# Gathering small products between longer dense runs, and a last output block scaled in three transfers

## The chip, the cores and the metric

The kernel runs on one core of one Trainium2 chip. The metric is the device time of one launch in microseconds. Before the change three runs took 757.4 to 757.57 us, with a median of 757.45.

Five engines work side by side, each through its own instructions in a fixed order: PE (TensorE, matrix products; PEld is its weight load), DVE (VectorE), ACT (ScalarE), POOL (GpSimd), and SP (SyncE), which issues nearly all transfers.

## The reference

One decoder layer over 512 tokens, with 16 meta tokens ahead of them (528 in all), a width of 1024, in float32. Attention with differential softmax (8 heads) and a chunked gated delta rule (8 heads) run side by side on the same normalised input:

```python
h = concatenate([meta, x])
hn = rms_norm(h, norm_w)
aq, ak, av, az, dq, dk, dv, dz, db, da, ga, gd = split(hn @ w_in)
# attention, two maps a head
p = softmax(causal(q k^T / 8));  o_a = (p[0] - lam * p[1]) @ v
y_a = (rms_norm(o_a) * c * silu(az)) @ w_branch_attn
# delta rule, chunks, each head
t_inv = inverse(unit lower triangle: m + eye)
u, w = t_inv @ (v * beta), t_inv @ (k * beta * exp(gc))
v_new = u_c - w_c @ state
o_c = qd_c @ state + a_c @ v_new
state = state * cd_c + kd_c^T @ v_new
y_d = (rms_norm(o_d) * silu(dz)) @ w_branch_delta
h = h + (sigmoid(ga) * y_a + sigmoid(gd) * y_d) @ w_out
out = rms_norm(h, final_norm_w)[meta tokens dropped]
```

## The kernel before

**Dense products.** The products with the big weights (`w_in`, the two branches, `w_out`) make most of PE's work. Operands are split into a high and a low part (`hnH`, `hnL`, `wh`, `wl`; for sums of blocks `sumH`, `sumL`), and each product is made as three passes, high x high, high x low, low x high (`PASSES`), with 256, 264 or 512 columns. The functions are `first_products`, `product`, `pair_of_blocks` and `pair_products`, called one after the other by the generator `dense`, and `rest_of_gates`.

**Small products.** Between dense passes stand fp32 products and transposes of 32 to 128 rows. They come from `attention` (its score products are dense passes; `combine` turns the softmax's two maps into one and multiplies by the values) and from `delta_pair`, which treats the heads of the delta rule in four pairs. Of a pair, `keys`, `values`, `products` and `queries` make operands; then the inverse of the unit triangles is solved on DVE for all diagonal blocks at once, in 62 dependent operations on `tmps` and `ts` (31 multiplications, 31 subtractions). What it reads comes through DRAM (`scrm`) into `room`; what it gives goes through `scrt` to `tds` and `tdms`. From `tdms` the meta tokens' block is transposed (`tdmt`), and PE multiplies `vrm` by it, which starts the state. `square` and others finish the inverse (`TM`, `MT`, the wide `TT`), and `steps` walks over the chunks: `kT` by the state `S`, on DVE `vin`, its product with `TT`, on ACT `u`, then `ktd` by `u` and on DVE the next `S`; `output` adds the queries' product and that of `u` with `AT`.

**What sets the order.** All order is made ahead of time by a planner (`Plan`). Each part of the work is a generator (a `Task`), which yields the engine it wants next, a slot of a buffer, or an event. `run` takes again and again the task that could begin first by the planner's own clock; of several, the one with the lower rank. Its clock adds up durations from `Engine.time`, latencies from one engine to another (`HOP`) and an estimate for transfers. The order in which tasks are taken is the order in which each engine executes. No engine steps past an instruction that waits: what stands behind it waits too. `delta_pair` runs at rank 0, ahead of the dense work in a tie.

**Buffers.** Six PSUM banks are shared by kinds (`pd` three, `pat` two, `pdl` two); other buffers have the counts in `SLOTS`.

**The end.** The last products are `project`, four blocks of 128 tokens by two halves of 512 columns. `finish` takes such a half from its bank: DVE adds the residual (into `xr`), ACT squares it and sums the squares, DVE weighs it by the final norm's weights (`weigh`, a task of its own of rank 2). When both halves of a block are there, POOL raises the mean square to -0.5, ACT scales the half o = 0 and DVE the half o = 1, and SP sends each out, 128x512 apiece. In the last block the second half is computed in two cuts of 256 columns.

All instructions that go through the helper `Engine` stand in the profile at its one line, L231, so groups and rows are told apart by their tiles.

Of the kernel before, what the change touches and what calls it, by code (L numbers as in the profile page):

```python
# [79 lines left out]
COLD = 10500  # L80


class Task:
    def __init__(self, gen, rank, time, src):
        self.gen, self.rank, self.time, self.src, self.want, self.slot = gen, rank, time, src, (), 0
        self.issued = None


class Plan:
# [9 lines left out]
    def __init__(self, slots, kinds, banks):  # L99
        self.free = dict.fromkeys((PE, DVE, ACT, POOL, SP), 0.0)  # L100
        self.slots = {k: [(0.0, SP, i) for i in range(n)] for k, n in slots.items()}
        self.slots["bank"] = [(0.0, SP, i) for i in range(banks)]
        self.kinds = dict(kinds)
        self.events, self.tasks = {}, []
        self.task, self.engine, self.end, self.arrival = None, None, 0.0, 0.0
        self.dma = self.hwdge = 0.0

    def here(self):

# [4 lines left out]
    def spawn(self, gen, rank=None):  # L114
        time, src = self.here() if self.task else (0.0, SP)
        self.tasks.append(Task(gen, self.task.rank if rank is None else rank, time, src))
# [21 lines left out]
    def transfer(self, nbytes):  # L138
# [2 lines left out]
        self.dma = max(self.dma, self.hwdge) + nbytes / 360 + 20  # L141
        self.arrival = self.dma + 900

    def resume(self, task, engine, begin):
        self.task, self.engine, self.end, self.arrival = task, engine, begin, 0.0
        task.want = next(task.gen, None)
        task.time, task.src = self.here()
        task.issued = self.end if self.arrival else None
        if engine:
            self.free[engine] = self.end  # L150
        if task.want is None:
            self.tasks.remove(task)
        self.task = self.engine = None
# [31 lines left out]
    def run(self):  # L185
        self.settle()
        while self.tasks:
            best = None
            for task in self.tasks:
                eng = task.want  # L190
                if isinstance(eng, tuple) or eng not in self.free:
                    continue
                t = task.time if task.issued is None or eng != SP else task.issued
                if task.src != eng:
                    t += self.HOP[task.src] + (80 if eng == PE else 0)
                elif eng in (DVE, ACT):
                    t += 130
                key = max(t, self.free[eng]), task.rank
                if best is None or key < best[0]:
                    best = key, task  # L200
            assert best, sorted({str(t.want) for t in self.tasks})
            self.resume(best[1], best[1].want, best[0][0])
            self.settle()


# [60 lines left out]
def hybrid_block(ctx: ExitStack, tc: tile.TileContext, x, meta, wblk, wbd, wout, pcol, prow, out):  # L266
# [45 lines left out]
    def tick(event, n):  # L312
        ticks[event] = ticks.get(event, 0) + 1
        if ticks[event] == n:
            done(event)
        return ticks[event] == n
# [670 lines left out]
    def delta_pair(gi):  # L987
# [258 lines left out]
        for o in range(4):  # L1246
# [2 lines left out]
            G.affine_select(out=part, in_=part, pattern=[[1, 32], [-3, 11]], base=-(o % 3),  # L1249
                            channel_multiplier=-1 if o == 3 else 0, compare_op=ALU.is_equal, fill=0.0)  # L1250
        yield name("scr")
        msub = room[1].rearrange("p a t -> p (a t)")[:, 0:D].rearrange("p (j i) -> p j i", i=32)
        for o in range(4):

# [258 lines left out]
    def attention(h):  # L1513
# [11 lines left out]
        def combine(i, st, es):  # L1525
            N = NM + P * (i + 1)
            yield DVE
            V.reciprocal(out=st[:, 5:6], in_=st[:, 4:5])
            yield DVE
            V.tensor_scalar(out=st[:, 6:7], in0=l0[:, i:i + 1], scalar1=st[:, 5:6], scalar2=nlam, op0=ALU.mult, op1=ALU.mult)  # L1530
            yield DVE
            V.scalar_tensor_tensor(out=es[0], in0=es[1], scalar=st[:, 6:7], in1=es[0], op0=ALU.mult, op1=ALU.add)
            give("e")

            yield ("pm",)
            which = plan.task.slot
            pm = late["pm"][which]
            yield ACT
            A.copy(out=pm[:, 0:2, 0:NM], in_=es[0][:, 0:NM].unsqueeze(1).broadcast_to([P, 2, NM]))
            yield DVE  # L1540
            V.tensor_tensor(out=pm[:, 2, 0:NM], in0=es[0][:, 0:NM], in1=pm[:, 0, 0:NM].bitcast(F32), op=ALU.subtract)
            yield ("pT",)
            pT, pmT = slot(ap, [P, NC, P], F32, "pT"), mk(ap, [96, P], F32R, "pmT", SLOTS["pT"])
            yield ("pat",)
            yield PE
            pt = bank("pat")
            for n in range(i + 1):
                T.transpose(pt[:, n * P:(n + 1) * P], es[0][:, chunk(n)], ident)
            give("e")
            w = (i + 1) * P  # L1550
            dst = pT[:, 0:i + 1, :].rearrange("p n q -> p (n q)")
            yield ACT
            A.copy(out=dst, in_=pt[:, :w])
            give("pat", pt)
            yield ("pat",)
            po = bank("pat")
            yield PE
            T.transpose(po[0:96, P:2 * P], pm.rearrange("p a t -> p (a t)").bitcast(F32), ident)
            plan.give("pm", which)
            yield ACT  # L1560
            A.copy(out=pmT, in_=po[0:96, P:2 * P])
            yield PE
            T.matmul(po[:, 0:P], pmT, late["vm"], start=True, stop=False)
            for n in range(i + 1):
                T.matmul(po[:, 0:P], pT[:, n, :], vs[:, n, :], start=False, stop=n == i)
            give("pT")
            yield ACT
            A.copy(out=o[:, i, :], in_=po[:, 0:P])
            A.activation(out=po[:, P:2 * P], in_=po[:, 0:P], func=AF.Square, accum_out=ss[:, i:i + 1])
            give("pat", po)  # L1570
            tick(f"ao{h}", NC)
# [52 lines left out]
        for c in range(NC):  # L1624
            yield ACT
            A.activation(out=o[:, c, :], in_=o[:, c, :], func=AF.Copy, scale=ss[:, c:c + 1])
        yield f"az{h}"
        yield ("pat",)
        yield PE
        pt = bank("pat")  # L1630
# [377 lines left out]
    def finish(hf, tb, c0, c1, pd, tag, ssq, fnw, xr):  # L2008
# [13 lines left out]
        def weigh():  # L2022
            yield DVE
            V.tensor_tensor(out=t, in0=t, in1=fnw[hf][:, c0:c1], op=ALU.mult)
            tick(f"fw{tb}", 3 if tb == NC - 1 else 2)

        spawn(weigh(), 2)

        if col == 0:
            yield DVE  # L2030
# [1 line left out]
        elif c1 == 512:  # L2032
# [4 lines left out]
            G.tensor_tensor(out=ssq[:, 4:5], in0=ssq[:, 4:5], in1=mhalf[:, 0:1], op=ALU.pow)  # L2037
            yield f"fw{tb}"

            def scale(o):  # L2040
                t = xr[o, tb]
                if o == 0:
                    yield ACT
                    A.activation(out=t, in_=t, func=AF.Copy, scale=ssq[:, 4:5])
                else:
                    yield DVE
                    V.tensor_scalar_mul(out=t, in0=t, scalar1=ssq[:, 4:5])
                yield SP
                S.dma_start(out=out[tb * P:(tb + 1) * P, 512 * o:512 * o + 512], in_=t)

            for o in range(2):
                spawn(scale(o))
        else:
            yield DVE
            V.scalar_tensor_tensor(out=ssq[:, 3:4], in0=ssq[:, col:col + 1], scalar=1.0 / D, in1=ssq[:, 3:4],
# [144 lines left out]
```

## Time and profile before

| | |
|---|---|
| median of 3 runs | 757.45 us |
| the profiled execution's own time | 757.24 us |
| span of its trace | 755.5 us |
| PE busy | 735.5 us, 97% of the span, 5311 instructions |
| PEld busy | 668.6 us, 88% |
| DVE busy | 626.2 us, 83% |
| ACT busy | 498.6 us, 66% |
| POOL busy | 74.7 us, 10% |
| granted clock of TensorE, mean | 0.997 of full |

The profile is of one execution; its time is 0.21 us below the median, and 1.74 us of it lie outside the span. A row of the trace has the start in us, the duration (of one instruction, or from the first's start to the last's end where several are drawn together as xN), the engine, the operation, what it writes and reads, and in brackets how long the engine stood still just ahead of it and for whom. In the view of stretches each row has the stretch, its length, then pairs of busy time and instructions for PE, PEld, DVE, ACT and POOL, then the granted clock, the share of the DMA engines and GB/s.

PE's matmuls are pipelined: the record of a pass lasts longer than the time from its start to that of the next one. That time from start to start is called a turn here: 0.12 us for a pass of 256 or 264 columns.

### The profile page before, as it was taken

Reading aid. Unit: us, or ns where it says so; the run is one execution under the profiler, and the core shown is the slowest. Engines: PE = TensorE matmul, PEld = TensorE weight load, DVE = VectorE, ACT = ScalarE, POOL = GpSimd, SP = SyncE. Lnnn points to the kernel's source line nnn. Section 1 sums busy time; section 2 is a strip of 40 time slices with the busy share of each in tenths; the row PEclk is TensorE's granted clock in tenths of the full one; section 3 lists DMA queues with packets and bytes.
Section 4 is the critical chain, followed back from the end, with each engine's and each line's share of the span. In section 5 each row is a group of like instructions: output and inputs, shape, how many; then the busy total and the mean of one; then the engine's idle time right before and its main releaser. Section 6 shows DMA issues by size and latency. Waiting matters only on the chain.

```text
span 755.5 us, 14370 instructions
## 1 busy us (share of the span) xinstructions
PE 735.5 (97%) x5311; PEld 668.6 (88%) x5311; DVE 626.2 (83%) x1431; ACT 498.6 (66%) x1322; POOL 74.7 (10%) x86
## 2 busy tenths in 40 slices
PE   5999999999999999999999999999999999999996
PEld 5998888899899899989989989988988998899875
DVE  6999999998889789879989888997479869797453
ACT  6369565879965678976767797767675445545132
POOL 3205000202000301100030210010000000000001
PEclk9999999999999999999999999999999999999998
DMA  8141321225314112521331152152141443132602
GB/s 306 57 133 33 114 80 64 64 71 158 97 42 140 34 53 85 169 78 52 110 79 59 36 180 85 56 202 65 49 147 57 141 130 121 56 118 90 239 4 109
DMA packets 45431, 74.88 MB, mean 99 GB/s; under 512 B 20728, under 2 KB 25636, under 8 KB 45360
## 3 DMA queue, kind: packets, MB, share of 16 engines
q1 hardware_dynamic: 45360, 73.95, 30.8%
q8 instruction: 42, 0.69, 0.4%
q14 instruction: 29, 0.24, 0.1%
HBM read 67.58 MB, written 6.36 MB: 98 GB/s over the span
## 4 chain that ended last, share of the span: by engine, by line
PE 83%; ACT 8%; DVE 4%; issue 2%; DMA 1%; POOL 0%; SPq 0%; POOLq 0%; ACTq 0%
PE bank L231 80%; PE psc L231 3%; ACT wh L231 2%; DVE wl L231 1%; ACT TM L231 1%; ACT ak L231 1%; DMA xt<-in_x_dram 1%; ACT vr L231 0%; DMA raw<-in_wblk_dram 0%; ACT bank L231 0%; ACT MT L231 0%; ACT e L231 0%; ACT aq L231 0%; ACT sqk L231 0%; DVE hnL L231 0%
## 5 line engine op out<-in xcount | busy, mean ns | idle before, releaser
L231 PE MATMUL bank<-hnH,wh 128*128 128x512 f32 (+4 forms) x664 | 233.4, 355 | 0.7 <-ACT hnH L231 0.7
L231 PE MATMUL bank<-hnH,wl 128*128 128x512 f32 (+4 forms) x664 | 221.6, 337 | 0.0
L231 PE MATMUL bank<-hnL,wh 128*128 128x512 f32 (+4 forms) x664 | 221.5, 337 | 0.0
L231 DVE TENSOR_TENSOR wl<-raw,wh 128x1024 fp32r<-128x1024 f32 (+1 forms) x120 | 134.9, 1126 | 24.6 <-ACT wh L231 24.1
L231 ACT CAST wh<-raw 128x1024 fp32r<-128x1024 f32 (+1 forms) x120 | 116.3, 971 | 43.4 <-PE bank L231 36.0
L231 PEld LDWEIGHTS bank<-hnH,wl 128*128 128x128 f32 x664 | 124.1, 188 | 13.9
L231 PEld LDWEIGHTS bank<-hnH,wh 128*128 128x128 f32 x664 | 124.5, 189 | 13.4 <-ACT hnH L231 0.9
L231 PEld LDWEIGHTS bank<-hnL,wh 128*128 128x128 f32 x664 | 124.4, 189 | 10.0
L231 PE MATMUL bank<-sumH,wh 128*128 128x264 f32 x224 | 68.5, 306 | 0.0
L231 PE MATMUL bank<-sumH,wl 128*128 128x264 f32 x224 | 63.6, 284 | 0.0
L231 PE MATMUL bank<-sumL,wh 128*128 128x264 f32 x224 | 63.5, 284 | 0.0
L231 DVE SCALAR_TENSOR_TENSOR y<-xp,pc,y 128x528 f32<-128x528 f32 (+1 forms) x72 | 54.0, 753 | 1.1 <-ACT y L231 1.0
L231 ACT ACTIVATE e<-psc,ast 128x144 f32<-128x144 f32 (+3 forms) x64 | 34.7, 543 | 21.5 <-DVE ast L231 18.3
L231 PEld LDWEIGHTS bank<-sumH,wh 128*128 128x128 f32 x224 | 42.3, 189 | 1.1 <-issue 0.6
L231 PEld LDWEIGHTS bank<-sumL,wh 128*128 128x128 f32 x224 | 42.4, 189 | 0.0
L231 PEld LDWEIGHTS bank<-sumH,wl 128*128 128x128 f32 x224 | 42.1, 188 | 0.0
L231 PE MATMUL bank<-btH,wh 128*128 128x256 f32 x128 | 36.1, 282 | 0.5 <-ACT sn L231 0.5
L231 PE MATMUL bank<-btH,wl 128*128 128x256 f32 x128 | 35.8, 280 | 0.0
L231 PE MATMUL bank<-btL,wh 128*128 128x256 f32 x128 | 35.8, 280 | 0.0
L231 ACT CAST wh<-st 128x1024 fp32r<-128x1024 f32 x22 | 23.1, 1048 | 13.0 <-PE bank L231 12.8
L231 PE MATMUL psc<-ak,aq 128*128 128x264 f32 (+3 forms) x160 | 29.7, 305 | 0.8 <-DVE aq L231 0.4
L231 DVE TENSOR_TENSOR wl<-st,wh 128x1024 fp32r<-128x1024 f32 x22 | 26.8, 1218 | 3.4 <-ACT wh L231 1.9
(373 smaller groups left out, 1699.5 us busy)
## 6 DMA issues: line engine op xcount, KB each, us to landing
raw<-in_wblk_dram SPq DMA_DIRECT2D x96, 512.0 KB, 3.5
raw<-in_wout_dram SPq DMA_DIRECT2D x8, 512.0 KB, 5.1
xt<-in_x_dram SPq DMA_DIRECT2D x4, 512.0 KB, 4.8
TM<-gcd SPq DMA_DIRECT2D x8, 256.0 KB, 5.2
xr<-in_x_dram SPq DMA_DIRECT2D x8, 256.0 KB, 6.3
out_dram<-xr SPq DMA_DIRECT2D x8, 256.0 KB, 2.5
room<-scrm SPq DMA_DIRECT2D x12, 128.0 KB, 3.3
oad<-room SPq DMA_DIRECT2D x6, 256.0 KB
```

The costliest lines, as they stand in the source:

```text
L231: return real(*args, **kw)
```

## The change

1. **The planner** (`Task`, `Plan`) learns which tasks are dense: those of the generators `dense`, `rest_of_gates` and `attention`, the last one only up to its closing transposes. When PE goes from small to dense work, 85 ns are added in the planner's clock (`SWITCH`). While a dense run lasts and another dense task is ready, a small product is not begun before the run has lasted 500 ns (rank 0) or 900 ns (`RUNS`). While small products run, a dense task is put 80 ns back in the comparison (`STAY`).
2. **`combine`**: of the sum over the values and the meta tokens' values, the meta tokens' product (`vm`, `pmT`) is made last; it was first.
3. **`delta_pair`**: the planner gets one more event to wait for, `t3`, before the fetch into `room`: a sum over token blocks, which lay in the same buffer, has then been split into its high and low part.
4. **`finish`**: the last 256 columns of the last block are no longer weighed by a task of their own; DVE weighs and scales them in one operation. The last block goes out in three transfers in place of two: the second half's first 256 columns, the first half, the last 256 columns.

The instructions of PE are the same in number and shape. POOL's and SP's are too, but for the one transfer more; DVE's end changes as under 4.

```diff
+DENSE = ("dense", "rest_of_gates", "attention")
+SWITCH, RUNS, STAY = 85, (500, 900), 80
 class Task:
+        self.other = False
 class Plan:
+        self.run_kind, self.run_since = False, 0.0
+    def dense(self, task):
+        return task.gen.__name__ in DENSE and not task.other
     def resume(self, task, engine, begin):
+        if engine == PE and self.dense(task) != self.run_kind:
+            self.run_kind, self.run_since = not self.run_kind, begin
+            begin += SWITCH * self.run_kind
     def run(self):
+            steady = self.run_kind and any(
+                t.want == PE and self.dense(t) and t.time + (t.src != PE) * (self.HOP[t.src] + 80) <= self.free[PE]
+                for t in self.tasks)
...
-                key = max(t, self.free[eng]), task.rank
+                if eng == PE and steady and not self.dense(task):
+                    t = max(t, self.run_since + RUNS[task.rank > 0])
+                begin = max(t, self.free[eng])
+                key = begin + STAY * (eng == PE and not self.run_kind and self.dense(task)), task.rank
                 if best is None or key < best[0]:
-                    best = key, task
+                    best = key, task, begin
-            self.resume(best[1], best[1].want, best[0][0])
+            self.resume(best[1], best[1].want, best[2])
...
         yield name("scr")
+        yield "t3"
         msub = room[1].rearrange("p a t -> p (a t)")[:, 0:D].rearrange("p (j i) -> p j i", i=32)
...
             yield PE
-            T.matmul(po[:, 0:P], pmT, late["vm"], start=True, stop=False)
             for n in range(i + 1):
-                T.matmul(po[:, 0:P], pT[:, n, :], vs[:, n, :], start=False, stop=n == i)
+                T.matmul(po[:, 0:P], pT[:, n, :], vs[:, n, :], start=n == 0, stop=False)
+            T.matmul(po[:, 0:P], pmT, late["vm"], start=False, stop=True)
...
         yield f"az{h}"
+        plan.task.other = True
...
-            tick(f"fw{tb}", 3 if tb == NC - 1 else 2)
-        spawn(weigh(), 2)
+            tick(f"fw{tb}", 2)
+        last = tb == NC - 1 and hf == 1 and c1 == 512
+        if not last:
+            spawn(weigh(), 2)
...
-            def scale(o):
-                t = xr[o, tb]
+            def scale(o, a, b):
+                t = xr[o, tb][:, a:b]
                 if o == 0:
                     yield ACT
                     A.activation(out=t, in_=t, func=AF.Copy, scale=ssq[:, 4:5])
+                elif last and a:
+                    yield DVE
+                    V.scalar_tensor_tensor(out=t, in0=t, scalar=ssq[:, 4:5], in1=fnw[o][:, a:b], op0=ALU.mult, op1=ALU.mult)
                 else:
                     yield DVE
                     V.tensor_scalar_mul(out=t, in0=t, scalar1=ssq[:, 4:5])
                 yield SP
-                S.dma_start(out=out[tb * P:(tb + 1) * P, 512 * o:512 * o + 512], in_=t)
+                S.dma_start(out=out[tb * P:(tb + 1) * P, 512 * o + a:512 * o + b], in_=t)
-            for o in range(2):
-                spawn(scale(o))
+            for o, a, b in ((1, 0, 256), (0, 0, 512), (1, 256, 512)) if last else ((0, 0, 512), (1, 0, 512)):
+                spawn(scale(o, a, b))
```

**The order at the steps over the chunks.** PE's order of before, in the first pair of heads (`u,AT` the output's second product, `S,kT` the next chunk's first, of the two heads in turn; `sumH`, `sumL` dense passes; the helper's line is L231 before and L252 now):

```order
L231 MATMUL bank_1_78<-u_1997,AT_1057 128x128
L231 MATMUL bank_2_79<-sumH_35_134,wh_23_120 128x264
L231 MATMUL bank_2_79<-sumL_39_138,wh_23_120 128x264
L231 MATMUL bank_2_79<-sumH_35_134,wl_24_121 128x264
L231 MATMUL bank_5_82<-S_2011,kT_549 128x128
```

Behind these rows stand once more the same three dense passes, and then the second head's `S,kT`. The same place in the changed kernel, with other dense passes beside it:

```order
L252 MATMUL bank_4_81<-u_1942,AT_1035 128x128
L252 MATMUL bank_2_79<-hnH,wh_19_116 128x264
L252 MATMUL bank_2_79<-hnL,wh_19_116 128x264
L252 MATMUL bank_2_79<-hnH,wl_20_117 128x264
L252 MATMUL bank_2_79<-hnH,wh_19_116 128x264
L252 MATMUL bank_2_79<-hnL,wh_19_116 128x264
L252 MATMUL bank_2_79<-hnH,wl_20_117 128x264
L252 MATMUL bank_5_82<-S_1961,kT_552 128x128
L252 MATMUL bank_6_83<-S_1964,kT_609 128x128
```

Six dense passes now stand in one run, and the two heads' small products together behind them. Over the whole order the runs of small products fall from 209 to 186, those of dense passes under 500 ns by the planner's clock from 37 to 4, and changes between products on a part and on the whole of PE's array from 92 to 90.

**The order at the solve's end.** In the first pair of heads, PE's product of `vrm` with the transposed `tdmt`, before:

```order
L231 MATMUL bank_5_82<-sumH_34_133,wl_20_117 128x264
L231 MATMUL bank_3_80<-vrm_673,tdmt_1612 32x128
L231 MATMUL bank_5_82<-sumH_34_133,wh_19_116 128x264
L231 MATMUL bank_5_82<-sumL_38_137,wh_19_116 128x264
L231 MATMUL bank_5_82<-sumH_34_133,wl_20_117 128x264
```

and now:

```order
L252 MATMUL bank_2_79<-hnH,wl_24_121 128x264
L252 MATMUL bank_4_81<-vrm_655,tdmt_1567 32x128
L252 MATMUL bank_6_83<-TM_662,MT_897 32x32 x4
L252 MATMUL bank_6_83<-TM_662,MT_962 32x32 x4
L252 MATMUL bank_6_83<-TM_662,MT_897 32x32 x4
L252 MATMUL bank_6_83<-TM_662,MT_962 32x32 x4
L252 MATMUL bank_5_82<-um_1669,ktm_654 128x128
```

The product was row 622 of PE's order and is row 589; small products of the same pair (`TM,MT` of `square`, `um,ktm` of the state) follow it at once, where dense passes did.

**The order in `combine`.** In one block of an attention head PE's order was, between two groups of dense passes:

```order
L231 MATMUL bank_3_80<-sumH_34_133,wh_23_120 128x264
L231 MATMUL bank_3_80<-sumL_38_137,wh_23_120 128x264
L231 MATMUL bank_3_80<-sumH_34_133,wl_24_121 128x264
L231 MATMUL bank_2_79<-vm_653,pmT_2898 128x128
L231 MATMUL bank_2_79<-vs_2623,pT_2897 128x128
```

and is now:

```order
L252 MATMUL bank_3_80<-sumH_36_135,wh_19_116 128x264
L252 MATMUL bank_3_80<-sumL_40_139,wh_19_116 128x264
L252 MATMUL bank_3_80<-sumH_36_135,wl_20_117 128x264
L252 MATMUL bank_6_83<-vs_2619,pT_2953 128x128
L252 MATMUL bank_6_83<-vm_635,pmT_2954 128x128
```

The product that needs ACT's copy `pmT` has changed places with that of the values, which needs the earlier copy `pT`.

## The prediction

> **What bounds the kernel now.** I read the page first: busy time, then the chain that ended last.
>
> ```profile
> span 755.5 us, 14370 instructions
> ...
> PE 735.5 (97%) x5311; PEld 668.6 (88%) x5311; DVE 626.2 (83%) x1431; ACT 498.6 (66%) x1322; POOL 74.7 (10%) x86
> ...
> PE 83%; ACT 8%; DVE 4%; issue 2%; DMA 1%; POOL 0%; SPq 0%; POOLq 0%; ACTq 0%
> ```
>
> PE is busy for 97% of the span and makes 83% of the chain. The change adds and removes no product: only time in which PE stands still can be won or lost. The table of stretches says where it stands still (time and instructions by engine; the first pair is PE).
>
> ```profile
> 30.00:530.00 500.00, 495.36 (x3816) 454.48 (x3817) 445.62 (x1105) 375.90 (x1086) 56.62 (x56) 1.00 0.29 89
> 530.00:748.90 218.90, 218.44 (x1350) 193.84 (x1349) 156.15 (x272) 106.90 (x206) 5.78 (x6) 1.00 0.32 105
> 748.90:755.50 6.60, 0.27 (x3) 0.07 (x1) 1.41 (x4) 1.23 (x3) 0.66 (x1) 0.70 0.31 117
> ```
>
> From 530 to 748.9 PE leaves 0.46 us, and the order of its work there is unchanged. Behind 748.9 lie 6.6 us of tail. From 30 to 530, where small products stand between dense ones, it leaves 4.64 us. The view of PE's waits in that stretch has eleven rows (what waited, for what, us, times, longest), 4.2 us in sum; these are the first, two that matter below, and the last:
>
> ```profile
> PE bank L231 <- DVE qT L231: 1.0, 2, 0.7
> ...
> PE bank L231 <- DVE tdmt L231: 0.4, 1, 0.4
> PE bank L231 <- DVE vin L231: 0.4, 1, 0.4
> ...
> PE bank L231 <- ACT cn L231: 0.2, 1, 0.2
> ```
>
> These understate it, since a matmul's record lasts longer than its turn. At the worst `vin`:
>
> ```profile
> 167.72 0.40 PE L231 MATMUL bank<-vin,TM 128*128 128x128 f32 x2
> 168.51 0.49 PE L231 MATMUL bank<-vin,TM 128*128 128x128 f32 x2 [0.39 <-DVE vin L231]
> ```
>
> A two-pass product takes 2 x 0.11 = 0.22 us of turn (pace below), the step is 0.79: 0.57 lost where the row says 0.39. With 0.18 more for each of the 13 named waits the pool is about 4.2 + 2.3 = 6.5 us.
>
> **The change part by part.** The sum is made against the profiled execution's own 757.24 us, 0.21 below the median 757.45.
>
> *Switches.* The planner now charges 85 ns whenever PE goes from small to dense products. Eight transposes between dense passes (start, length):
>
> ```profile
> 49.46 0.28 PE L231 MATMUL bank<-hnH,wl 128*128 128x256 f32 x1
> 49.58 1.04 PE L231 MATMUL bank<-ident,kT 128*128 128x128 f32 x8
> 50.37 0.36 PE L231 MATMUL bank<-hnH,wh 128*128 128x256 f32 x1
> 50.57 0.28 PE L231 MATMUL bank<-hnL,wh 128*128 128x256 f32 x1
> 50.69 0.28 PE L231 MATMUL bank<-hnH,wl 128*128 128x256 f32 x1
> ```
>
> The first dense record behind them is 0.08 longer (0.36 against 0.28), which looks like a price. By starts it is none: from 49.46 to 50.57 are 1.11 us, and one dense turn, eight of 0.11 and one dense make 0.12 + 0.88 + 0.12 = 1.12. [...] Only a product on a part of the array pays:
>
> ```profile
> 149.99 0.68 PE L231 MATMUL bank<-TM 64*64 64x64 f32 x8
> 150.59 0.39 PE L231 MATMUL bank<-hnH,wh 128*128 128x264 f32 x1
> 150.82 0.28 PE L231 MATMUL bank<-hnL,wh 128*128 128x264 f32 x1
> ```
>
> Eight records spread over 0.68 - 0.22 = 0.46 us are 0.06 each; 8 x 0.06 + 0.12 = 0.60, and 0.83 pass: 0.23. In the order, runs of small products fall from 209 to 186, but changes between a part and the whole of the array only from 92 to 90. So: 23 x 0 + 2 x 0.12 = **-0.2**, from 0 to 23 x 0.085 = -2.0.
>
> *Gathering.* At the steps over the chunks PE has six dense passes and then both heads' products, where it had three dense passes between the two (rows of PE's order, above). That lengthens some covers and shortens others. I add the paces along the order between a product and the one that needs its result. For `vin` the smallest cover rises from 0.44 to 0.89 us, but the median falls from 1.46 to 1.17; from `vin` to `u,ktd` the median goes from 1.17 to 1.25. Links with less cover than the shortest time that this kind of link took in the trace: 38 before, 32 now. I take **-1.0**, from -4 (over half of the pool) to +1.5 (the `vin` links late by 0.05 each).
>
> *Meta tokens' product behind.* It waited for ACT's copy `pmT`, here 131.12 - 130.82 - 0.12 = 0.18:
>
> ```profile
> 130.82 0.28 PE L231 MATMUL bank<-hnH,wl 128*128 128x264 f32 x1
> 131.12 0.33 PE L231 MATMUL bank<-vm,pmT 96*128 96x128 f32 x1
> ```
>
> Now `vs,pT`, which has its operands earlier, stands ahead with 0.22 a block. By such steps three or four of 32 blocks waited: **-0.4**, from 0 to -0.7.
>
> *The solve.* Each pair of heads solves its triangle on DVE: 62 dependent operations between DMAs, ended by a transpose for which PE's product `vrm,tdmt` waits; behind that, in order, all of PE's work. The first four rows are the DVE chains (own busy time last), the others the stretches on PE from the last `kT` product to `vrm,tdmt`:
>
> ```profile
> 89.33:128.40 39.07, 13.78 (x62) 1.00 0.25 82
> 212.58:255.20 42.62, 13.64 (x62) 1.00 0.21 69
> 345.53:384.90 39.37, 13.77 (x62) 1.00 0.23 75
> 472.91:506.70 33.79, 13.93 (x62) 1.00 0.37 127
> ...
> 72.29:136.68 64.39, 62.58 (x406) 55.97 (x404) 60.64 (x153) 40.23 (x99) 5.86 (x6) 1.00 0.30 86
> 198.33:263.56 65.23, 65.19 (x442) 59.72 (x441) 57.51 (x156) 44.18 (x120) 6.74 (x9) 1.00 0.24 67
> 331.96:392.46 60.50, 60.50 (x413) 55.32 (x411) 56.45 (x156) 39.44 (x114) 6.28 (x7) 1.00 0.29 82
> 458.81:514.40 55.59, 55.59 (x374) 50.57 (x372) 51.27 (x143) 36.35 (x100) 2.15 (x3) 1.00 0.35 109
> ```
>
> Before, other DVE rows inside the chains last 30.9, 36.8, 31.6 and 23.1 us by their own durations; in the new order 29.3, 29.3, 32.8 and 33.3. The chains took 0.87 of own plus others (154.9 of 177.5), so they change by -1.4, -6.5, +1.0 and +8.8. PE's work by paces on the same stretches was 61.0, 64.7, 59.9 and 55.3 and is now 59.8, 56.4, 57.5 and 59.6: -1.3, -8.3, -2.4, +4.3. Chain minus cover: -0.1, +1.8, +3.4, +4.5. There was next to no reserve except in pair 3:
>
> ```profile
> 513.34 0.19 DVE L231 STREAM_TRANSPOSE tdmt<-tdm 32x32 f32<-32x32 f32 x1
> ...
> 514.39 0.40 PE L231 MATMUL bank<-vrm,tdmt 32*32 32x128 f32 x2
> ```
>
> 514.39 - 513.53 = 0.86 of reserve there; pair 0 waited (the `tdmt` row above). So PE is late by up to 1.8 + 3.4 + 3.7 = 8.9 us, and at best wins back 0.8, which pairs 0 and 1 wait now. In pair 0 that product stands 33 rows earlier in PE's order, and where a dense pass followed it, now the 32x32 products follow at once: a little more of PE's work hangs on the transpose. Other DVE work that falls into gaps of the chain costs nothing (in pair 3 DVE stood idle for 55.59 - 51.27 = 4.3), so I take under a third of the upper end: **+2.5**, from -0.8 to +8.9.
>
> *Tail.*
>
> ```profile
> 750.35 0.42 DVE L231 TENSOR_TENSOR xr<-xr,fnw 128x256 f32<-128x256 f32 x1
> 750.51 0.66 POOL L231 TENSOR_TENSOR ssq<-ssq,mhalf 128x1 f32<-128x1 f32 x1 [4.20 <-DVE ssq L231]
> 751.21 0.72 ACT L231 ACTIVATE xr<-xr,ssq 128x512 f32<-128x512 f32 x1 [0.97 <-POOL ssq L231]
> 751.21 0.49 DVE L231 TENSOR_SCALAR xr<-xr,ssq 128x512 f32<-128x512 f32 x1 [0.44 <-POOL ssq L231]
> 751.72 0.81 SPq L231 DMA_DIRECT2D out_dram<-xr  x2
> ```
>
> The weighing that goes (0.42) ended at 750.77, beside POOL's power (to 751.17): nothing. DVE then has a half scaling, between 0.16 and 0.49, say 0.33, and 0.42: ready at 751.54 and 751.96, ACT's at 751.93. SP issues in 0.81 / 2 = 0.40 each: 751.57, 751.97, 752.37. The last issue is 0.25 later than now and carries half the bytes: **0**, from -0.4 to +0.4. The wait on `t3` is for a sum on DVE that was long done when the fetch went out: 0; uncovered it would delay that fetch, and with it the chain of a pair, by one sum, about the 1.1 us of this row:
>
> ```profile
> L231 DVE TENSOR_TENSOR wl<-raw,wh 128x1024 fp32r<-128x1024 f32 (+1 forms) x120 | 134.9, 1126 | 24.6 <-ACT wh L231 24.1
> ```
>
> Sum: -0.2 - 1.0 - 0.4 + 2.5 + 0 = +0.9: 758.1 us; against the median 757.45 + 0.9 = 758.3.
>
> **Rivals.**
>
> *Covered (faster).* The longer runs take most of the short waits, and DVE's fillings fall into gaps: -0.2 - 4.0 - 0.6 + 0.5 = -4.3: 753.1. For it: 38 falls to 32, the smallest `vin` cover doubles. Against it: the median of `vin` falls.
>
> *The solve late (slower).* PE's cover for the transpose is short by two thirds of the upper end, +6, less 1 of short waits: 762.4. It decides from 1 us a pair. For it: no reserve in pairs 0 to 2, and the 85 ns are charged 76 times on these four stretches (6.5 us) though full-array rows show no such price. Against it: before, the planner hit this product to within 0.9 us in all pairs.
>
> *It does not gather.* 209 to 186 runs is little, and the waits stay as they are: 757.2.
>
> **How the numbers follow.** Forecast 0.42, covered 0.27, late 0.21, no gathering 0.10. What measurement of this kernel tells from no change is about 0.2%, 1.5 us. The forecast's own spread (-2.5 to +4) puts 0.05 faster, 0.20 same and 0.17 slower; covered 0.26 faster, 0.01 same; late all slower; no gathering 0.01 faster, 0.09 same. Faster 0.32, same 0.30, slower 0.38. The range 752.8 to 763.5 leaves out the outer part of both rivals.
>
> **What would show it.** PE idle from 30 to 530 against 4.64 us; the rows of waits for `tdmt` (right: 2 to 4 us over the four pairs; under 1 us and the solve step is wrong); waits for `vin` and `u`, smaller in number; `pmT` gone; dense turns still 0.12 across a switch; the last issue near 752.4 less the shift of the span. Wrong altogether if another engine holds PE: a new long wait for `wl`, `xp` or `vT`.

## The result, and the profile after

The changed kernel takes 770.83 us (median of 4 runs, 767.92 to 771.0); the kernel before took 757.42 beside it. The ratio is 1.0168 (95% interval 1.0144 to 1.0192): 13 us slower. The profiled execution took 770.9, in a span of 769.2. The page of after, the same three parts as before the change (busy time, chain):

```profile
span 769.2 us, 14348 instructions
...
PE 742.8 (97%) x5311; PEld 671.4 (87%) x5311; DVE 625.7 (81%) x1431; ACT 498.1 (65%) x1322; POOL 75.0 (10%) x86
...
PE 58%; DVE 23%; ACT 10%; issue 4%; DMA 2%; POOL 1%; SPq 1%; DVEq 0%; POOLq 0%; ACTq 0%
```

PE has the same work and is "busy" 7.3 us longer; its share of the chain falls from 83% to 58%, and DVE's rises from 4% to 23%. The view of stretches, cut at the same places of the program as before (500, 218.9 and 6.6 us then):

```profile
30.00:543.60 513.60, 503.44 (x3839) 458.96 (x3838) 445.53 (x1109) 376.58 (x1096) 57.06 (x56) 0.99 0.29 86
543.60:762.60 219.00, 218.54 (x1331) 193.21 (x1331) 155.95 (x268) 105.87 (x198) 5.75 (x6) 1.00 0.32 106
762.60:769.20 6.60, 0.35 (x4) 0.15 (x2) 1.33 (x4) 1.23 (x3) 0.55 (x1) 0.83 0.26 94
```

All of the loss lies in the first one: 13.6 us. PE's idle time there is 513.60 - 503.44 = 10.16, against 4.64: 5.5 more. The other 8.1 are in PE's "busy" time. PE's waits in that stretch, the five longest of twelve rows, which make 9.8 us in sum (what waited, for what, us, times, longest):

```profile
PE bank L252 <- DVE tdmt L252: 3.6, 3, 1.5
PE bank L252 <- DVE vT L252: 1.1, 3, 0.5
PE bank L252 <- DVE xp L252: 1.1, 2, 0.9
PE bank L252 <- ACT ao L252: 0.9, 2, 0.5
PE psc L252 <- ACT e L252: 0.8, 3, 0.3
```

About half of those 8.1 shows in the column of the granted clock (third from the end) in fine stretches behind the solve of the first pair of heads:

```profile
132.00:134.00 2.00, 1.18 (x10) 0.76 (x8) 2.00 (x4) 2.00 (x9) 0.00 (x0) 1.00 0.00 0
134.00:136.00 2.00, 1.60 (x36) 1.37 (x35) 1.92 (x6) 1.94 (x6) 0.00 (x0) 0.86 0.68 178
136.00:138.00 2.00, 2.00 (x8) 1.77 (x9) 1.67 (x3) 1.89 (x6) 0.00 (x0) 0.50 0.24 92
...
144.00:146.00 2.00, 2.00 (x12) 2.00 (x12) 0.86 (x3) 0.85 (x3) 0.00 (x0) 0.58 0.18 70
146.00:148.00 2.00, 2.00 (x25) 1.77 (x24) 0.50 (x2) 1.63 (x2) 0.00 (x0) 1.00 0.00 0
```

For 10.2 us (135.44 to 145.68) TensorE ran at half its clock, which never happened in the profile of before between 30 us and its last products. What stands just ahead of it on PE (start, length):

```profile
132.53 0.28 PE L252 MATMUL bank<-hnH,wl 128*128 128x264 f32 x1
133.64 0.40 PE L252 MATMUL bank<-vrm,tdmt 32*32 32x128 f32 x2 [0.82 <-DVE tdmt L252]
133.98 1.09 PE L252 MATMUL bank<-TM,MT 32*32 32x32 f32 x32
135.01 0.48 PE L252 MATMUL bank<-um,ktm 32*128 32x128 f32 x2
135.88 0.79 PE L252 MATMUL bank<-um,ktm 32*128 32x128 f32 x2 [0.40 <-DVE um L252]
136.60 0.59 PE L252 MATMUL bank<-hnH,wh 128*128 128x264 f32 x1
```

From 132.65 to 136.60 PE has nothing but products on 32 of the array's 128 rows, with two stalls between. They are the gathered products of the solve's hand-over; in the order of before dense passes stood between them. The three runs that took 770.76 or more had a mean clock of 0.992, the one that took 767.92 had 0.997. So there are two losses to tell apart: waits, and the clock.

### The profile page after: what moved, and what is told of

It is laid out like the page before. It is cut to its first block, busy times and chain, and to the rows that moved or that the text cites. A ratio compares the mean times of both kernels' runs of the same rounds, so it can differ in the third digit from the quotient of the medians.

```text
span 769.2 us, 14348 instructions
## 1 busy us (share of the span) xinstructions
PE 742.8 (97%) x5311; PEld 671.4 (87%) x5311; DVE 625.7 (81%) x1431; ACT 498.1 (65%) x1322; POOL 75.0 (10%) x86
## 4 chain that ended last, share of the span: by engine, by line
PE 58%; DVE 23%; ACT 10%; issue 4%; DMA 2%; POOL 1%; SPq 1%; DVEq 0%; POOLq 0%; ACTq 0%
PE bank L252 56%; DVE wl L252 6%; PE psc L252 3%; DVE y L252 2%; ACT wh L252 2%; DVE ts L252 2%; DVE tmps L252 2%; DVE ast L252 2%; ACT TM L252 1%; DVE raw L252 1%; ACT e L252 1%; DVE ak L252 1%; DMA xt<-in_x_dram 1%; DVE qT L252 1%; DVE vT L252 1%
## 5 line engine op out<-in xcount | busy, mean ns | idle before, releaser
L252 PE MATMUL bank<-hnH,wh 128*128 128x512 f32 (+4 forms) x664 | 233.2, 354 | 3.0 <-DVE vT L252 1.1
L252 PE MATMUL bank<-hnH,wl 128*128 128x512 f32 (+4 forms) x664 | 222.1, 338 | 0.0
L252 PE MATMUL bank<-hnL,wh 128*128 128x512 f32 (+4 forms) x664 | 222.0, 338 | 0.0
L252 ACT CAST wh<-raw 128x1024 fp32r<-128x1024 f32 (+1 forms) x120 | 116.2, 971 | 45.8 <-PE bank L252 42.9
L252 DVE TENSOR_TENSOR wl<-raw,wh 128x1024 fp32r<-128x1024 f32 (+1 forms) x120 | 134.2, 1120 | 11.5 <-ACT wh L252 10.8
L252 PEld LDWEIGHTS bank<-hnH,wh 128*128 128x128 f32 x664 | 125.0, 190 | 17.0 <-DVE vT L252 2.2
L252 PEld LDWEIGHTS bank<-hnH,wl 128*128 128x128 f32 x664 | 124.7, 189 | 13.9
L252 PEld LDWEIGHTS bank<-hnL,wh 128*128 128x128 f32 x664 | 125.0, 190 | 9.5
L252 PE MATMUL bank<-sumH,wh 128*128 128x264 f32 x224 | 68.1, 304 | 0.1
L252 PE MATMUL bank<-sumL,wh 128*128 128x264 f32 x224 | 64.5, 288 | 0.0
L252 PE MATMUL bank<-sumH,wl 128*128 128x264 f32 x224 | 64.4, 287 | 0.0
L252 DVE SCALAR_TENSOR_TENSOR y<-xp,pc,y 128x528 f32<-128x528 f32 (+1 forms) x72 | 54.8, 762 | 0.5 <-ACT y L252 0.5
L252 ACT ACTIVATE e<-psc,ast 128x144 f32<-128x144 f32 (+3 forms) x64 | 34.5, 542 | 20.7 <-DVE ast L252 13.9
L252 PEld LDWEIGHTS bank<-sumH,wh 128*128 128x128 f32 x224 | 43.2, 193 | 0.5 <-ACT vT L252 0.3
L252 PEld LDWEIGHTS bank<-sumL,wh 128*128 128x128 f32 x224 | 43.3, 193 | 0.0
L252 PEld LDWEIGHTS bank<-sumH,wl 128*128 128x128 f32 x224 | 43.0, 192 | 0.0
L252 PE MATMUL bank<-btH,wh 128*128 128x256 f32 x128 | 36.3, 284 | 0.5 <-ACT sn L252 0.5
L252 PE MATMUL bank<-btH,wl 128*128 128x256 f32 x128 | 36.0, 281 | 0.0
L252 PE MATMUL bank<-btL,wh 128*128 128x256 f32 x128 | 35.9, 281 | 0.0
L252 ACT CAST wh<-st 128x1024 fp32r<-128x1024 f32 x22 | 23.1, 1050 | 12.5 <-PE bank L252 12.4
L252 PE MATMUL psc<-ak,aq 128*128 128x264 f32 (+3 forms) x160 | 29.7, 305 | 1.2 <-ACT e L252 0.8
L252 DVE TENSOR_TENSOR wl<-st,wh 128x1024 fp32r<-128x1024 f32 x22 | 26.9, 1221 | 2.6 <-ACT wh L252 2.5
```

The lines of the kernel that those rows point to most:

```text
L252: return real(*args, **kw)
```

## The experiments

Each ran beside the kernel before on the same chip; times are medians, and in brackets stands the ratio to the kernel before with its 95% interval. The first four ask which part of the change it is. The theory: the planner's three numbers, and of them SWITCH, by which the planner believes PE slower than it is and puts products ahead of their operands. The rival: the gathering (RUNS, STAY) bares the small chains.

**rest_only**

```diff
-SWITCH, RUNS, STAY = 85, (500, 900), 80
+SWITCH, RUNS, STAY = 0, (0, 0), 0
```

> The change with SWITCH = 0, RUNS = (0, 0), STAY = 0: only the meta tokens' product behind, the planner's wait for t3 and the tail of the last block are left. Theory (all of the 13 us come from the planner's three numbers): 756.5 to 757.6 us, clock 0.997. Rival (the meta tokens' product or the tail cost something): 758.5 or more, with new waits for pT or a later last transfer.

762.07 us (1.0062, 1.0042 to 1.0082), at clocks of 0.985 to 0.995. Both were wrong in part: without the planner's three numbers, with PE's order of before but for the meta tokens' products, 4.6 us are lost, and not by waits for `pT` or the end. The trace has them in one place, the second pair's hand-over:

```profile
266.55 1.09 PE L252 MATMUL bank<-TM,MT 32*32 32x32 f32 x32 [1.23 <-ACT TM L252]
```

and behind it, in the view of stretches:

```profile
266.00:268.00 2.00, 1.46 (x36) 1.40 (x36) 2.00 (x6) 1.96 (x8) 0.00 (x0) 1.00 0.40 133
268.00:270.00 2.00, 2.00 (x15) 1.73 (x13) 1.60 (x4) 1.92 (x6) 0.00 (x0) 0.87 0.32 129
270.00:272.00 2.00, 2.00 (x34) 1.87 (x36) 0.83 (x3) 1.71 (x4) 0.00 (x0) 0.50 0.34 131
```

One wait of 1.23 us in such a place, and the clock fell to 0.50. The wait goes back to POOL: its four selects on `ts` took 4.36 us there, 3.27 in the kernel before, while DVE's `wl` beside them took 1.23 us here and 1.75 before. So POOL's `ass` was late by 0.9, ACT behind it too, its `TM` among that, and PE. The length goes with the order: the selects took 4.32 us in warm_rest, which has the same order, and 3.27 and 3.29 in tail_only and late_handoff, which have that of before.

**switch_only** and **no_switch**

```diff
-SWITCH, RUNS, STAY = 85, (500, 900), 80
+SWITCH, RUNS, STAY = 85, (0, 0), 0
```

> SWITCH = 85 with RUNS = (0, 0), STAY = 0: the planner believes each switch to dense work to cost 85 ns, and gathers nothing (202 runs of small products, against 209 before and 186 in the change). PE's product vrm,tdmt stands 46, 61, 101 and 24 matmuls earlier than before. Theory A (the 85 ns bring small products forward, ahead of the results that they wait for): 763 to 770 us, waits for tdmt of 3 us or more, as in the change. Theory B (the gathering uncovers the small chains): within 1.5 us of the kernel before.

```diff
-SWITCH, RUNS, STAY = 85, (500, 900), 80
+SWITCH, RUNS, STAY = 0, (500, 900), 80
```

> SWITCH = 0 with RUNS = (500, 900), STAY = 80: gathered as in the change (184 runs of small products), but vrm,tdmt stands within 10 matmuls of its old place in all four pairs. Theory A: 755 to 759 us, no wait for tdmt over 0.6, clock 0.997. Theory B: 764 us or more; the stretch of 32-row products in the first pair and the drop of the clock behind it are still there.

772.57 us (1.0198, 1.016 to 1.0236) and 759.85 (1.0027, 1.0017 to 1.0037; clock 0.997 to 0.999). SWITCH without the gathering loses 15 us, over theory A's range, and the gathering without SWITCH 2.4, a little over it. In switch_only PE waits 3.4 us for `tdmt`, in no_switch 1.0.

**no_stay**

```diff
-SWITCH, RUNS, STAY = 85, (500, 900), 80
+SWITCH, RUNS, STAY = 85, (500, 900), 0
```

> STAY = 0, SWITCH and RUNS as in the change: a dense pass may come between small products at once (188 runs). Theory A: 763 to 771 us, since vrm,tdmt stands 38, 49, 76 and 38 matmuls earlier than before. Theory B, with STAY as the part that leaves the solve's products bare: under 762 us, clock 0.997 and no stretch of small products alone.

764.28 us (1.0091, 1.0073 to 1.0108). Within the theory's range, at its lower end; it says little by itself.

The next five ask whether the fall of the clock is a cause, and what the new end costs.

**warm_after**, **warm_rest** and **warm_three**: transposes that nobody reads, put on PE into stalls.

```diff
+            for _ in range(8 if gi == 0 else 0):
+                nc.tensor.transpose(pm[:, 2 * P:3 * P], ident, ident)
             T.matmul(pm[0:32, 0:P], tdmt, vrm, start=True, stop=True)
...
+                for _ in range(4 if gi == 0 and i else 0):
+                    nc.tensor.transpose(pm[:, 2 * P:3 * P], ident, ident)
                 T.matmul(pm[:, P * i:P * (i + 1)], ktm, um[i], start=True, stop=True)
```

> The changed kernel with its orders as they are, and in the first pair of heads 12 transposes of the identity more on PE, whose results nobody reads: eight ahead of vrm,tdmt, where PE stands still for over 1 us, and four between the two um,ktm products, where it stands still for about 0.4. At 0.11 us each they fill time that is lost anyway. Theory (PE's clock falls to half because the array has next to nothing to do for over 3 us there): clock 1.00 behind 134 us, 766.5 to 768.5 us. Rival (the clock falls for another reason, or its fall costs nothing that the waits don't cost): 770 us or more.

771.73 us, from 767.31 at a clock of 0.999 to 776.13 at 0.985. Inconclusive as a time: in the profiled run the clock stayed at 1.00 behind the first pair, but fell behind the third pair's hand-over, which it had passed in the change (the last section has a reading of why).

> The kernel rest_only with eight such transposes in the second pair of heads, ahead of the TM,MT product that waited 1.2 us for ACT there. Theory: no fall of the clock behind 267 us, 757.5 to 759.5 us. Rival (that pair's loss is the wait and not the clock): 760.5 us or more.

758.26 us (1.0013, 1.0001 to 1.0025), against 762.07 for rest_only. Eight idle transposes win 3.8 us. PE's rows, and the stretch behind them:

```profile
265.36 1.03 PE L1389 MATMUL bank<-ident 128*128 128x128 f32 x8
266.74 1.09 PE L252 MATMUL bank<-TM,MT 32*32 32x32 f32 x32 [0.34 <-ACT TM L252]
...
268.00:270.00 2.00, 2.00 (x16) 1.71 (x15) 1.59 (x4) 1.92 (x6) 0.00 (x0) 1.00 0.45 184
```

ACT's `TM` is as late as in rest_only (PE's `TM,MT` group starts at 266.74 and 266.55, in a trace that is 0.2 us later in all): what differs is that the stall is filled, and the clock stayed at 1.00. Here the clock is shown to be the cause.

> warm_after with idle transposes in three pairs: eight, 12 and 14 ahead of vrm,tdmt in the first, second and third pair (it stood still 1.2, 1.8 and 2.0 us there) and the four between the um,ktm products of the first. Theory (the fall of the clock makes about 3 us of the median's loss and the scatter of the runs; waits make the other 10): clock 0.997 or more in nearly all runs, 767 to 768.5 us, runs within 2 us of each other. Rival (the clock falls at other places all the same, so it is no matter of these hand-overs): 770 us or more, scattered as before.

768.0 us (1.0129, 1.0112 to 1.0145), all four runs between 767.35 and 768.71, at 0.997 or 0.999. So 2.8 us of the median are the clock, and some 10 us are not; the change's own run of 767.92 at 0.997 agrees. For the profiled execution the clock's price can be read from the same products in both traces, from `vrm,tdmt` of the first pair to the `TM,MT` group of 64 rows; first the change, then warm_three:

```profile
133.64 0.40 PE L252 MATMUL bank<-vrm,tdmt 32*32 32x128 f32 x2 [0.82 <-DVE tdmt L252]
146.76 0.27 PE L252 MATMUL bank<-TM,MT 64*64 64x64 f32 x1
```

```profile
135.23 0.40 PE L252 MATMUL bank<-vrm,tdmt 32*32 32x128 f32 x2
144.23 0.27 PE L252 MATMUL bank<-TM,MT 64*64 64x64 f32 x1
```

13.12 us against 9.00, with four idle transposes in the second: 4.1 us for one fall.

**tail_only**: the kernel before with the new `finish` and nothing else.

> The kernel before with the new end alone (the last 256 columns weighed as they are scaled, three transfers). PE's order is that of before. Forecast of the prediction's step: within 0.4 us of the kernel before, the last transfer issued about 0.25 us later and landing about as late. Rival (the three transfers win or lose a landing): 0.5 us or more either way.

757.24 us beside 757.55 (0.9993, 0.9984 to 1.0001): no more than 0.3 us won, and not clear of nothing.

**late_handoff**: the kernel before with a late transpose in the second pair.

```diff
+            for _ in range(8 if gi == 1 else 0):
+                nc.vector.transpose(out=tdmt, in_=tdm)
             V.transpose(out=tdmt, in_=tdm)
```

> The kernel before with eight repeats of the transpose tdmt<-tdm ahead of the real one, in the second pair of heads alone: the hand-over from the solve comes later by about 1 us (0.1 to 0.19 us each), PE's order is unchanged. Theory (every stall of 1 us in that place also halves the clock behind it): 761 us or more, clock under 0.997. Rival (a late hand-over costs its own length): 758 to 759 us.

760.75 us (1.0038, 1.0019 to 1.0058), from 758.62 at 0.999 to 765.16 at 0.99. The eight took 1.82 us, more than I said. A late hand-over costs 1.1 us in the fastest run, at 0.999 (758.62 - 757.55), and up to 7.6 in the slowest, at 0.99. Neither expectation is the whole.

The next six ask whether SWITCH hurts by its size, or whether any new order would have lost.

```diff
             slow = 2 if self.name == PE and self.plan.end < COLD else 1
+            slow *= 1.02 if self.name == PE else 1
```

> The kernel tail_only, ordered by a planner that believes every PE instruction to last 2% longer (over the whole program about as much as the 85 ns at 186 switches, 15.8 us), with no SWITCH, RUNS or STAY; vrm,tdmt stands 49, -7, 57 and 29 matmuls earlier than before. Theory (a planner whose PE is slower than the real one brings small products forward, and they wait): 762 to 770 us. Rival (the loss comes from charging at switches, by which it is the runs that are rearranged): within 2 us of tail_only.

766.88 us (1.012, 1.0101 to 1.0138). Without `t3` this order puts the four fetches ahead of the operation that takes the low part of the third token sum, so that part is made of what the fetch brought, and the numbers that this kernel gives are not the layer's; PE's work is the same. PE waits 5.3 us in one place for `kT`, and the clock fell behind it: 0.62 is its mean from 434 to 443 us.

> The same with every PE instruction 1.5% shorter in the planner's belief. Theory: small products stand later or as before and their waits shrink, 755.5 to 758 us. Rival (the order of before is a pick among many, and any other order loses): 760 us or more, with waits as numerous as in the change.

764.11 us (1.0082, 1.0067 to 1.0097) with 0.985 in place of 1.02, at clocks of 0.997 to 0.999. Here the theory failed: a planner that errs to the other side loses 6.6 us too, by waits in other places (`AT` 1.1, `e` 1.0, `MT` 1.0, `sn` 0.9).

> The change with SWITCH = 40 in place of 85. Theory: the loss grows with the size of the wrong price, so between no_switch (759.85) and the change (770.83): 762 to 767 us. Rival (any new order loses by chance): no relation to the two, under 760 or over 769 us.

761.13 us (1.004, 1.0025 to 1.0055), a little under the theory's range, clocks from 0.993 to 0.997.

> The change with SWITCH = 20. Theory (the loss grows with the price charged): between no_switch and switch_40, 759.5 to 761.5 us. Rival (each new order is a draw, whatever the price): outside of it, by 1.5 us or more.

765.05 us (1.0092, 1.0077 to 1.0107). PE waits 4.8 us in one place for `kT`.

> The change with SWITCH = 60. Theory: between switch_40 (761.13) and the change (770.83), 763 to 769 us. Rival (a draw): outside of it.

758.9 us (1.0007, 0.9992 to 1.0021), from 756.88 at 0.997 to 761.39 at 0.99. With 0, 20, 40, 60 and 85 the times are 759.85, 765.05, 761.13, 758.9 and 770.83. They do not rise with the size: the theory of the wrong price fell in that form, and the rival, a draw at each new order, stands. With one order at each size, some effect of the size isn't excluded.

> The change with SWITCH = 0 and the meta tokens' product first again, as before: the gathering by RUNS and STAY, t3 and the new end. Theory (gathering at a right price neither wins nor loses much): 756.5 to 760 us, clock 0.997 or more. Forecast of the prediction's step (gathering wins 1 us, the end nothing): 756.5. Rival (the gathering itself uncovers chains): 761 us or more.

760.22 us (1.0033, 1.002 to 1.0045) at 0.997 to 0.999: in this order the gathering, with the new end, loses 2.7 us.

The last three hold the clock in two of these orders.

> switch_40 with the 12 idle transposes in the first pair of heads, where its clock fell (PE stood still 0.8 us for tdmt, 0.4 for TM and 0.6 for um there). Theory: 757 to 759 us at a clock of 0.997 or more, so that what was left of the loss of switch_40 was the clock. Rival: 760.5 us or more.

761.71 us (1.005, 1.0031 to 1.0069): not held, 0.995 and less.

> warm_40 with 22 idle transposes in the place of 12: four more ahead of TM,MT and six more around um,ktm. In warm_40 the clock still fell; PE's own work, weighed by the rows of the array that it uses, made 0.23 of the busiest-less 3.4 us there, against 0.37 and more in all traces in which it did not fall. Theory (a share of the array's work decides): the clock stays, 758 to 759.5 us. Rival (the clock falls at this place whatever PE does): 760.5 us or more at 0.995.

760.69 us (1.0043, 1.0029 to 1.0056), at 0.997 and 0.998 in three of four runs, and the trace of the fourth, at 0.995, is at half clock only in the start (18.4 us) and the tail: the clock holds at the hand-over, but 22 transposes take 2.4 us and the stalls did not cover all of it.

```diff
+            for _ in range((5, 3)[i] if gi == 0 else 0):
+                nc.tensor.transpose(pq[:, 2 * P:3 * P], ident, ident)
```

> switch_60 with eight idle transposes in the first pair of heads, ahead of its last TM products (five and three), where PE stood still 0.7 us and the clock fell behind. Theory (switch_60 loses by the clock alone; its fastest run, at 0.997, took 756.88): 757.0 to 757.8 us at a clock of 0.997 or more, runs within 2 us, which is level with the kernel before or 0.1% under it. Rival: 758.5 us or more, scattered as switch_60.

757.05 us beside 757.32 (0.9999, 0.999 to 1.0008), all but two of eleven runs between 756.89 and 757.29. The stretch where the clock fell, switch_60 and then warm_60:

```profile
148.00:150.00 2.00, 2.00 (x18) 1.88 (x17) 1.90 (x4) 0.79 (x2) 0.00 (x0) 0.50 0.00 0
150.00:152.00 2.00, 2.00 (x11) 2.00 (x10) 0.95 (x3) 0.89 (x2) 0.00 (x0) 0.50 0.00 0
152.00:154.00 2.00, 2.00 (x11) 1.99 (x11) 1.92 (x4) 1.64 (x3) 0.00 (x0) 0.50 0.00 0
```

```profile
148.00:150.00 2.00, 2.00 (x19) 2.00 (x18) 2.00 (x6) 1.63 (x3) 0.00 (x0) 1.00 0.00 0
150.00:152.00 2.00, 2.00 (x20) 2.00 (x19) 1.99 (x4) 1.51 (x7) 0.00 (x0) 1.00 0.00 0
152.00:154.00 2.00, 2.00 (x20) 1.98 (x19) 2.00 (x7) 1.64 (x7) 0.37 (x1) 1.00 0.76 256
```

It is the best version with the planner's change, and level with the kernel before: the planner's change, in a lucky order and with the clock held, wins nothing that can be measured.

## Why the prediction was wrong

It forecast +0.9 us, with a range up to 763.5; +13.4 was measured. Two steps failed. The sum had no term for TensorE's clock, which was left at the 1.00 of the rows of before: its fall cost 4.1 us of the profiled execution. And the gathering with the meta tokens' product, put at -1.4, did not shorten the waits outside the solve: they grew by 3.2. The solve's term was besides too small by 1.1. Going through the sum:

- **Switches, -0.2.** Not isolated. The runs with other sizes of SWITCH scatter by 12 us with the order that comes out, so a price of this size can't be seen in them.
- **Gathering, -1.0: failed, also in sign.** PE's waits but those for `tdmt` went from 3.8 to 6.2 us by the records, and with the prediction's 0.18 for each of 12 and now 17 of them from 6.0 to 9.2. With SWITCH at 0 (no_switch) they are 4.4 by the records, so most of the growth came with the order that SWITCH = 85 gives. The step counted covers along chains (38 short links, now 32), and those chains did well: in the change the wait for `vin` is 0.2 and `u` is not in the view. What waits now is what I had not counted, and a sign that the prediction had named for being wrong altogether: new waits for `xp` and `vT`, 1.1 us each. One is a dense pass that needs a bank which DVE empties behind a long `wl` (start, length; DVE, then PE):

```profile
308.36 1.22 DVE L252 TENSOR_TENSOR wl<-raw,wh 128x1024 fp32r<-128x1024 f32 x1
309.50 0.77 DVE L252 TENSOR_TENSOR xp<-bank,cn 128x264 f32<-128x264 f32 x2
...
308.83 0.28 PE L252 MATMUL bank<-sumH,wl 128*128 128x264 f32 x1
309.98 0.39 PE L252 MATMUL bank<-hnH,wh 128*128 128x264 f32 x1 [0.87 <-DVE xp L252]
```

What gathering does to the time differs with the order that it meets. gather_only loses 2.7 us, but no_switch takes 2.2 less than rest_only, where the gathering is added to an order in which the clock fell, and the change 1.7 less than switch_only, within their intervals.

- **Meta tokens' product behind, -0.4: failed in rest_only's order.** `pmT` is gone from the waits of the change, as forecast. But rest_only, which has this product, the tail and the wait on `t3` alone, loses 4.6, of which 3.8 go with the fall of the clock behind POOL's longer selects. With the clock held (warm_rest) it is 0.7 over the kernel before, idle transposes included, where -0.4 was said.
- **The solve, +2.5: the sum was near, in part by luck.** The wait for `tdmt` went from 0.4 to 3.6 us by the records, within the 2 to 4 that were named as proof, and by 3.6 with the 0.18 for each. But by pairs the waits are 0.8, 1.3, 1.5 and none, where up to -0.1, +1.8, +3.4 and +3.7 were argued: the pair that was to be latest does not wait, and the first waits twice as long as before. The chains went from 39.07, 42.59, 39.29 and 33.78 us to 38.41, 36.42, 38.85 and 38.51, that is by -0.7, -6.2, -0.4 and +4.7, where -1.4, -6.5, +1.0 and +8.8 were argued. Part of what was late came behind the chain: from its end to the transpose's end it took 8.2, 8.3, 7.6 and 6.8 us, and takes 8.8, 9.2, 8.7 and 9.2. In the third pair ACT's copies had ended by 382.71, and the transpose started at 384.55, since DVE's order had other work first:

```profile
382.41 0.30 ACT L252 COPY tdm<-tdms 32x30 f32<-32x30 f32 x2
...
382.31 1.03 DVE L252 TENSOR_TENSOR raw<-raw,raw 128x512 f32<-128x512 f32 x1
383.27 0.75 DVE L252 TENSOR_SCALAR l<-l 128x4 f32<-128x4 f32 x1
383.85 0.69 DVE L252 TENSOR_TENSOR ak<-vT,ak 64x528 fp32r<-64x528 f32 x1
384.47 0.15 DVE L252 SCALAR_TENSOR_TENSOR ass<-ass,l 128x4 f32<-128x4 f32 x1
384.55 0.19 DVE L252 STREAM_TRANSPOSE tdmt<-tdm 32x32 f32<-32x32 f32 x1
```

- **Tail, 0: right.** Behind the last matmul (its start) 6.63 us passed before (748.89 to 755.52), and 6.53 pass now (762.67 to 769.2); tail_only says the same.
- **What had no term: the clock.** One fall costs 4.1 us in the profiled execution and 2.8 in the median. The prediction read the column of the granted clock, found 1.00 and took it as given. It even noted that the 32x32 products follow at once now, and asked only what waits for them, not what the array does meanwhile.

The account of the 13.6 us in the profiled execution: 4.1 the clock; the waits' records went from 4.3 to 9.8 us, and with the prediction's 0.18 for each of 13 and now 20 of them, from 6.6 to 13.4: 6.8, of which 3.6 for `tdmt` and 3.2 for all else. The 0.18 is an estimate from one row. Some 2.7 us are left without a name, and their cause is open.

Of the rivals, "the solve late" (762.4, +5 with the other terms) was nearest, and too small. The largest error stands behind all terms: each took the order of before as the middle of what a planner gives. Of the ten orders that other numbers gave the planner, the change's among them, only that of switch_60 came level with it. The chance of slower should have been far larger than 0.38 for that alone. That is shown as a scatter; why the order of before is so good is open.

## What to carry to other kernels

A planner's order is one draw: give a new rule several seeds or sizes and measure the scatter before its mean is believed, since here a change from 60 to 85 in one constant cost 12 us. When small products are gathered, look at what is left of the array's work over the next few microseconds, not only at what waits: two stalls of 0.8 and 0.4 us by the records, about a run of 32-row products, cost 4 us more through the clock. And at a hand-over between engines ask for the place in the queue of every engine on the way, not only for when the operand is there.

## What the runs showed of the hardware

**In these traces the clock fell behind stretches with little work, not only behind empty ones.** The clock's changes lie on a grid. In the trace of the change it rises at 12.56 us (the turn of a transpose goes from 0.21 to 0.11 us there), falls at 135.44, rises at 145.68 and falls in the tail at 766.91: 36, 39 and 221 times 3.41333 us behind the first. In the trace of before it rises at 14.22 and falls in the tail at 751.50, 216 times 3.41333 behind. In these two traces no change is more than 2 ns off such a multiple; in the views of the other runs the stretches at half clock between 30 us and the last products are 3.4 or 6.8 us long, within 0.1 of one or two such steps. Where the grid lies against the program differs between the two: the first rise comes at 12.56 and at 14.22 us.

I added up PE's turns in each window of this grid (from a matmul's start to the next one's, at most its usual turn), each weighed by its share of the array's 128 rows. In the window ahead of the fall, 132.03 to 135.44, five dense passes make 0.61 us, and four 128-column turns of 0.11 us with 32 records over 1.03 us, all on 32 rows, about (0.4 + 1.0) x 1/4 = 0.35: some 0.28 of the window. In the eleven falls between 30 us and the last products, in ten traces, this share was 0.00 to 0.43. Of the 4,200 other windows there at full clock four had 0.41 to 0.42, and none had less; the kernel before has 0.52 at its lowest. Over 3.4 us in any other position the share does not tell falls from none (no_stay had 0.23 without a fall), so the 0.37 in the expectation of warm_40_more does not hold. In the change PE's records fill 2.78 of the 4 us from 132 to 136 (1.18 and 1.60 in the fine stretches of the first section), and the clock fell at 135.44 all the same.

So the same wait cost the clock in one trace and not in another. The third pair's hand-over, first the change, then warm_after:

```profile
384.79 0.40 PE L252 MATMUL bank<-vrm,tdmt 32*32 32x128 f32 x2 [1.50 <-DVE tdmt L252]
```

```profile
382.80 0.40 PE L252 MATMUL bank<-vrm,tdmt 32*32 32x128 f32 x2 [1.51 <-DVE tdmt L252]
```

In the change the grid's point at 384.62 cuts the stall in two, the windows on its sides have shares of 0.54 and 0.50, and the clock stayed. In warm_after all of the stall lies in the window from 379.96 to 383.38, its share is 0.43, and the clock fell at 383.38. That runs of one kernel differ fits this, but each kernel has one trace, so it isn't shown.

**Two small operations of DVE took over four times as long beside POOL's selects.** In the third pair of the change two of DVE's small operations on `l` ran beside POOL's selects (379.32 to 383.99 us): one at 381.32 us, which took 669 ns, and one at 383.27, which took 754. The view of the first kind (shortest, median, longest in ns):

```profile
L252 DVE TENSOR_TENSOR l<-l x8: 143/154/669, 153.0 to 551.9; 128x4 f32<-128x4 f32 x8
```

In the kernel before the longest were 162 and 171. Not every operation beside the selects (257.75 to 261.02 us there) took longer: `ass<-ass,l` at 259.34 us took 0.16 us, its median in that trace. The selects prepare the next pair's `ts` as soon as the last one has been sent off, so they fall near the hand-over, where DVE's queue holds the transpose. No run here moved the selects, so what they cost the change isn't shown.
